# Hybrid mixer layer on one core: unstepped transposes by permuted weights, and another precedence for the decays and the first branch

## The chip, the cores and the metric

The kernel runs on one core of a Trainium2 chip. The core has a matrix engine (TensorE, "PE" in the profile, with its weight loads as "PEld"), a vector engine (VectorE, "DVE"), a scalar engine (ScalarE, "ACT"), a general engine (GpSimd, "POOL") and a queue that issues most DMAs (SyncE, "SP"). They run side by side and wait for each other through semaphores. The metric is the device time of one execution in microseconds (us); lower is better.

## The reference

One layer of a decoder on 512 tokens of 1024 channels: a gated feed-forward network (FFN), a mixer, a second FFN, a norm. All arithmetic is float32.

```python
h = x + 0.5 * swiglu(rmsnorm(h, ffn1_norm), ...)
h = h + hybrid_mixer(rmsnorm(h, mix_norm), ...)
h = h + 0.5 * swiglu(rmsnorm(h, ffn2_norm), ...)
y = rmsnorm(h, final_norm)

# hybrid_mixer
proj = u @ w_in      # hq hf hi hg | gq gk gv ga gb gz | gate_h gate_g
o_h = hgrn2_chunked(silu(hq), k_h, hi, log_f)                     # 8 heads of 128
o_h = rmsnorm(o_h, hgrn_out_norm) * silu(hg)
y_h = o_h @ w_branch_hgrn
o_g = gated_delta_chunked(q_g, k_g, cv, beta, g)                  # 16 heads of 128
o_g = rmsnorm(o_g, gdn_out_norm) * silu(gz)
y_g = o_g @ w_branch_gdn
y = sigmoid(gate_h) * y_h + sigmoid(gate_g) * y_g
return y @ w_out
```

Both branches normalise each head's 128 output channels, scale them by a gain per channel, gate them and project them back to 1024 channels. The order of the channels inside a head is free, as long as the gain, the gate and the rows of the projection use the same one.

## The kernel before

**Layout.** Activations lie with channels on the 128 partitions and tokens along the free side ("transposed"). Weights come in slabs of 128 x 512 float32; each slab is loaded into a `raw` buffer, ACT rounds it to a high part (`whi`, line 1972 in the mixer) and VectorE takes the remainder (`wlo`, line 1974). Each product is three matmuls (lines 166 to 168): high by high, high by low, low by high. A projection block of the mixer is two slabs, eight k-steps and 24 matmuls of 128 x 512.

**Stages.** The first FFN, the mixer (`mixer`), then the second FFN. In the mixer the dense work (projections of the normed input) is woven with two recurrences that run head by head:

- The first branch (HGRN2, `h_head`, eight heads i = 0 to 7): per head the gates (`h_q`, `h_f`), seven levels of products on chunks of 128 tokens (event `("S", i)` when they are done), then the chunk recurrence, squares of the output on ACT (line 1208), a scale by the norm on VectorE (line 1218, event `("o", i)`), then the output is transposed to channels on partitions and split into a high part `oh` (line 1240, ACT) and a low part (line 1243, VectorE), event `("O", i)`. For heads 4 to 7 TensorE transposes (line 1228, `pt`). For heads 0 to 3 VectorE transposes 32 x 32 blocks (`turned`, line 913), the result goes to DRAM and comes back regrouped (`regroup`, line 933). The products y0 to y7 ("branch", 8 blocks with the weights `wbh`) use all eight heads as their k-steps, in the order of the heads.
- The second branch (gated delta rule, eight pairs u = 0 to 7 of value heads): the decays of a pair (`g_e`: a broadcast DMA `gb`, eight Abs on ACT at line 1315, two Exp at line 1320), the norms of q and k (`norms`, `g_n`), the gram products (line 1385), the inverse of a triangular matrix (`g_b` on POOL, `g_inv` with matmuls at lines 1474, 1484, 1497, 1505 and copies such as line 1477 on ACT between them), the chunk recurrence (`g_rec`), then the outputs: `send` for pairs 0 to 6 (fourteen heads, VectorE transposes at line 1627, to DRAM), `keep_on` for the last pair (TensorE transposes). `operand` brings the fourteen heads back regrouped, multiplies by the gain and the gate z (line 1724) and splits. `closing` multiplies the 16 heads with `wbg`, `merged` gates and adds the two branches, and the output projection `wo` follows.

**The stepped transpose.** VectorE transposes 32 x 32 blocks. Before, the source is read with `strided`: block b takes channels b, b+4, b+8 and so on, a step of four floats. After the way through DRAM, partition 4s + b then holds channel 4s + b, the natural order.

**What sets the order of the work.** Nothing in the mixer is scheduled by the hardware's readiness: a planner (class `Desk`) runs at build time and writes the instructions of all engines in one order. Each piece of work is a generator thread with a rank; it yields the engine it needs and a cost in us (`V(n)` = 0.21 + 0.001 n for VectorE, 1.05 for a stepped transpose), a wait for events (`"on"`), a buffer (`"get"`) or a lag. At each step the planner takes, on the engine that is free first, the ready thread with the lowest rank, or with a given priority such as the trailing 1 of `yield *V(550), 1`. Each engine then executes its instructions in exactly this order, and a real delay of one instruction holds up everything behind it on that engine.

The dense blocks are taken in the order of `DENSE`; `choose` (called each time a block's first `raw` buffer is free) takes the first block whose needs are met, and z and t gates when none is. `product` then issues the blocks on TensorE in the order in which they were chosen. It has rank 9, so it fills what the heads leave; but inside a block it waits for its operands, y blocks for event `("O", k)` at step k.

Of the kernel before, what the change touches and what calls it, by code (L numbers as in the profile page):

```python
# [12 lines left out]
ALU = mybir.AluOpType  # L13
# [3 lines left out]
P = 128  # L17
T = 512
NT = T // P
D = 1024  # L20
# [6 lines left out]
VH = 16  # L27


C_F1, C_MX, C_F2, C_FN, C_HN, C_GN, C_LB, C_CV = 0, 8, 16, 24, 32, 33, 34, 50  # L30
C_N = C_CV + 32 * 4
LEVELS = (1, 2, 4, 8, 16)

DENSE = (
# [782 lines left out]
def mixer(tc, mp, e):  # L817
    nc = tc.nc
    pe, act, dve, pool, sp = nc.tensor, nc.scalar, nc.vector, nc.gpsimd, nc.sync
# [29 lines left out]
    for size, names in ((1024, "n2:2 gz:2 fs:1 ut:1"), (512, "kn:3 gm:1 qm:2 gb:2 ln:1 at:4 vb:4 t64:2 on:2"),  # L849
                        (256, "ft:1 tp:1 thg:2 x:1 we:1 s:3 w:1"), (128, "fm:1"), (64, "sm:4")):  # L850
        for it in names.split():
            n, b = it.split(":")
# [36 lines left out]
    ohd = dr.tile([HH, P, T], F32, name="ohd")  # L889
# [16 lines left out]
        return places[tag](name, shape)  # L906


    def turned(x, src, mem, then=None, *arg):


        yield "use", "DVE", 1.05
        dve.transpose(squares(x), strided(src))
        if then is not None:
            then(*arg)
        yield S
        sp.dma_start(mem, x)
        yield "lag", LAG["out"]

    def squares(x):  # L920

        return x.rearrange("p (b c s) -> p c b s", b=4, c=NT)

    def strided(x):

        x = v3(x, NT) if len(x.shape) < 3 else x
        return x.rearrange("p c (s b) -> p c b s", b=4)
# [139 lines left out]
    def h_head(i):  # L1067
# [155 lines left out]
        if i >= 4:  # L1223
            yield "get", "d", 1
            yield T_(.46)
            x = ps("pt")
            for c in range(NT):
                pe.transpose(x[:, c * P:(c + 1) * P], on[:, c], ident)
        else:
            yield "get", "ta", 1  # L1230
            x = ta("xo")
            yield from turned(x, on, ohd[i], D.put, tag_o)
            yield from regroup(x, ohd[i])
        gn = cs[:, C_HN:C_HN + 1]
        o2 = op[i]("oh", (P, 2, T), F32R)
        oh, ol = o_h[i] = o2[:, 0], o2[:, 1]
        o4 = lambda z: z.rearrange("p (c b s) -> p c b s", c=NT, b=4)
# [63 lines left out]
    def g_e(u, st):  # L1301

        yield "on", "decays", *([("at", 2 * u + 1)] if u < 2 else ["more"]), *([*R(u - 4)] if u > 3 else []), \
            *([("E", u - 1)] if u else [])
        for i in range(2):
            hd_ = 2 * u + i
            yield "get", "gb", 1
            yield S
            gb = places["gb"]("gb", (P, NT, P))
            sp.dma_start(gb, gtd[hd_:hd_ + 1].rearrange("o (c b) -> o c b", c=NT).to_broadcast([P, NT, P]))  # L1310
            yield "lag", LAG["gb"]
            a = G["at"][u % 4 * 2 + i]
            for c in range(NT):
                yield A(200)
                act.activation(a[:, c], gb[:, c], AF.Abs, bias=gam[:, c, hd_:hd_ + 1], scale=-1.0)
            D.put("gb")
        yield "use", "ACT", 3.9
        for i in range(2):
            a = G["at"][u % 4 * 2 + i]
            act.activation(a, a, AF.Exp, scale=-1.0)  # L1320
        D.fire(("E", u))
# [301 lines left out]
    def send(u, i, o):  # L1623
        yield "get", "on", 1
        x = places["on"]("on")
        yield "use", "DVE", 1.05
        dve.transpose(squares(x), strided(o))
        D.fire(("R", u, i))
        D.start((6, u), keep(od[2 * u + i], x, "on", ("od", 2 * u + i)))

# [78 lines left out]
    def operand(k, wait, get, make):  # L1709

        yield "on", *wait
        if get:
            yield "get", get, 2
        yield "on", ("od", k), *(["projected"] if k > 10 else [])
        yield "on", ("z", k)
        tag = "zo" if k > 1 else "ta"
        yield "get", tag, 1
        yield "get", "ta", 1
        og, zg = ta("og"), zos.pop(0) if k > 1 else ta("zo")
        yield S  # L1720
        sp.dma_start(zg, zd[k])
        yield from regroup(og, od[k])
        yield *V(560), 1
        dve.scalar_tensor_tensor(og, og, cs[:, C_GN:C_GN + 1], zg, op0=ALU.mult, op1=ALU.mult)
        if k > 1:
            zos.append(zg)
        D.put(tag)
        if k > 8:
            yield "on", "projected"
        yield *A(512), 1  # L1730
        a, b = so[k] = make()
        a4, b4 = (z.rearrange("p (c b s) -> p c b s", c=NT, b=4) for z in (a, b))
        act.copy(a4, squares(og))
        yield *V(512), 1
        dve.tensor_tensor(b4, squares(og), a4.bitcast(F32), op=ALU.subtract)
        D.put("ta")
        D.fire(("so", k))
# [158 lines left out]
    def choose():  # L1896
        under = sum(("f", x) in D.at and x not in D.at for x in convs)
        for x in todo:
            k, i = x
            need = {"Q": [("Q", i - 2), ("F", i - 2), *([("o", i - 4)] if i > 3 else [])] if i > 1 else [], "F": [("L", i - 4)] if i > 3 else [],  # L1900
                    "B": [("pair", i - 2)] if i > 1 else [], "D": [], "S": [],
                    "y": [("O", 5), ("o", 6), ("S", 7)], "z": ["decays"],
                    "v": ["decays"],
                    "q": [("I", i - 4)] if i > 3 else ["decays" if i < 3 else "more"],
                    "k": [("I", i - 4)] if i > 3 else ["decays" if i < 3 else "more"]}[k]
            if k == "F" and i > 5:
                need = need + [("o", i - 6)]
            if all(n in D.at for n in need) and not (k in "qkv" and under >= CONVS):
                todo.remove(x)
                return x  # L1910
        return gates.pop(0) if len(gates) > (KEEP if todo else 0) else None
# [223 lines left out]
    D.start((6, 0), second())  # L2135
    D.start((6, 0), more())
    for u in range(8):
        D.start((4, u), g_e(u, st[u]))
        D.start((4, u), g_n(u, st[u]))
        D.start((4, u, 2), g_w(u, 0, st[u]))  # L2140
        D.start((4, u, 3), g_w(u, 1, st[u]))
        D.start((3, u), g_inv(u, st[u]))
        D.start((2, u), g_rec(u, st[u]))
# [30 lines left out]
def _cols(w):  # L2174

    k, n = w.shape
    return np.ascontiguousarray(w.reshape(k // P, P, n // P, P).transpose(2, 1, 0, 3)).reshape(n // P, P, k)
# [7 lines left out]
def layout(i):  # L2185
    f = {k: np.asarray(v) for k, v in i.items()}
    x = f["x"].reshape(T, D)
    per = lambda v: v.reshape(-1, P).T
    conv = f["gdn_conv_w"][0]
    cst = np.concatenate([  # L2190
        per(f["ffn1_norm"][0]), per(f["mix_norm"][0]), per(f["ffn2_norm"][0]), per(f["final_norm"]),
        per(f["hgrn_out_norm"][0]), per(f["gdn_out_norm"][0]),
        per(f["hgrn_lb_logits"][0]), per(f["hgrn_lb_logits"][1]),
        conv.reshape(4, 32, P).transpose(2, 1, 0).reshape(P, 128)], axis=1)
    a = np.arange(P)
    sqc = np.stack([np.eye(P), a[:, None] <= a[None, :], a[None, :] < a[:, None]], 1)
    hmask = np.zeros((P, 9, 64))
    for l, hh in enumerate(LEVELS):
        g, b = np.divmod(np.arange(64), hh)
        hmask[:, l] = (a[:, None] >= 2 * hh * g) & (a[:, None] < 2 * hh * g + hh)  # L2200
    eye4 = np.eye(32).reshape(32, 8, 4).transpose(2, 0, 1)
    hmask[:, 5:] = np.tile(np.repeat(eye4, 8, axis=0), (4, 1, 1)).reshape(P, 4, 64)
    w_in = f["w_in"][0]
    off = np.cumsum([0, 1024, 1024, 1024, 1024, 1024, 1024, 2048, 16, 16, 2048, 1024, 1024])
    part = [w_in[:, off[j]:off[j + 1]] for j in range(12)]
    wt = np.concatenate([_cols(part[j]) for j in (0, 1, 4, 5, 6, 10, 11, 9)])
    vg = np.stack([_pairs(part[j]).reshape(4, P, KD, 256) for j in (2, 3)], 3)
    wn = vg.reshape(4, P, 2, 2048).transpose(0, 2, 1, 3).reshape(8, P, 2048)
    wab = np.zeros((D, 64), np.float32)
    wab[:, 0:16] = part[7]  # L2210
    wab[:, 32:48] = part[8]

    def ffn(n):
        wi, wo = f[f"ffn{n}_w_in"][0], f[f"ffn{n}_w_out"][0]
        c = _cols(wi)
        return np.stack([c[:KF], c[KF:]], 1), _cols(wo)
    w1a, w2a = ffn(1)
    w1b, w2b = ffn(2)
    out = dict(
        xT=_kpn(x.T), cst=cst, sqc=sqc, hmask=hmask,  # L2220
        dta=np.stack([f["gdn_dt_bias"][0], f["gdn_a_log"][0]], 1),
        w1o=w1a[:2].reshape(4, P, KD, P).transpose(2, 1, 0, 3).reshape(KD, P, 512),
        w1a=w1a, w2a=w2a, wm=wt[[8, 0, 9, 1]].reshape(4, P, KD, P).transpose(2, 1, 0, 3).reshape(KD, P, 512),
        wt=wt, wn=wn, wab=_kpn(wab).reshape(P, -1),
        wbh=_cols(f["w_branch_hgrn"][0]), wbg=_cols(f["w_branch_gdn"][0]), wo=_cols(f["w_out"][0]),
        w1b=w1b, w2b=w2b)
    return {k: np.ascontiguousarray(v, dtype=np.float32) for k, v in out.items()}

# [14 lines left out]
```

## Time and profile before

| what | us |
|---|---|
| median of 3 runs | 1603.14 (1601.59 to 1603.28) |
| the profiled execution, its device time | 1604.23 |
| its span, first to last instruction | 1602.4 |
| TensorE busy | 1577.6 (98%) |
| VectorE busy | 1098.7 (69%) |
| ScalarE busy | 871.8 (54%) |
| GpSimd busy | 394.0 (25%) |

All times in the text count from the first instruction of the span. "Busy" leaves out waiting and DMA-issuing instructions. Rows of groups give an instruction's line, engine, operation, the tile that it writes and those that it reads (out<-in), and its count; rows of waits name the waiting instruction, the one that released it, and total, count and longest in us. The granted clock of TensorE is 1.00 at full speed.

### The profile page before, as it was taken

What the parts mean: (1) busy time and instruction counts of PE and PEld (TensorE: products, weight loads), DVE (VectorE), ACT (ScalarE), POOL (GpSimd) and SP (SyncE); (2) the same over time, 40 slices, a digit from 0 to 9 for tenths busy, and PEclk for the clock granted to TensorE, in tenths of its full rate; (3) what the DMA queues carried; (4) which work ended last, traced back from release to release, by engine and by line L of the source; (5) the groups of instructions that cost most, each with busy time, mean ns of one, the idle gap of its engine ahead of it and who ended that gap; (6) DMA issues with size and microseconds to landing.
All of it is one profiled execution on the core that took longest, in us unless ns stands there. A gap on an engine that the chain in (4) does not pass through costs nothing.

```text
span 1602.4 us, 29214 instructions
## 1 busy us (share of the span) xinstructions
PE 1577.6 (98%) x10586; PEld 1370.3 (86%) x10586; DVE 1098.7 (69%) x1982; ACT 871.8 (54%) x1905; POOL 394.0 (25%) x736
## 2 busy tenths in 40 slices
PE   8999999999999999999999999999999999999997
PEld 7999998888878778788878888888888899999887
DVE  7877775547778768747878776556546777778243
ACT  7766664334335446447676576555325776666232
POOL 0222210100222211172541744620002322220011
PEclk9999999999999999999999999999999999999999
DMA  5988842543323225564554646746645887872343
GB/s 178 237 187 184 184 109 83 181 119 93 103 64 93 81 78 145 148 197 142 160 174 151 207 142 186 218 150 198 204 132 166 207 200 184 185 171 73 118 140 114
DMA packets 175009, 243.72 MB, mean 152 GB/s; under 512 B 40320, under 2 KB 67712, under 8 KB 174864
## 3 DMA queue, kind: packets, MB, share of 16 engines
q1 hardware_dynamic: 157296, 210.16, 42.3%
q0 software_dynamic: 17280, 31.46, 12.5%
q8 instruction: 83, 1.36, 0.3%
q14 instruction: 62, 0.51, 0.1%
q10 hardware_dynamic: 288, 0.22, 0.0%
HBM read 211.08 MB, written 30.70 MB: 151 GB/s over the span
## 4 chain that ended last, share of the span: by engine, by line
PE 60%; DVE 1%; issue 1%; DMA 1%; ACT 1%; POOL 0%; SPq 0%; POOLq 0%; DVEq 0%; ACTq 0%
PE pmm L166 13%; PE pmm L167 13%; PE pmm L168 13%; PE pfa L167 2%; PE pfa L168 2%; PE pfa L166 2%; PE pfy L168 1%; PE pfx L166 1%; PE pfy L167 1%; PE pfy L166 1%; PE pfx L167 1%; PE pfx L168 1%; PE pgq L1385 1%; PE pw L1572 1%; PE pog L1588 1%
## 5 line engine op out<-in xcount | busy, mean ns | idle before, releaser
L166 PE MATMUL pmm<-uh,whi 128*128 128x512 f32 x760 | 317.7, 418 | 5.8 <-ACT whi L709 5.7
L168 PE MATMUL pmm<-uh,wlo 128*128 128x512 f32 x760 | 298.6, 393 | 0.0
L167 PE MATMUL pmm<-ul,whi 128*128 128x512 f32 x760 | 298.5, 393 | 0.0
L1972 ACT CAST whi<-raw 128x512 fp32r<-128x512 f32 x230 | 142.6, 620 | 257.5 <-PE pmm L167 189.4
L1974 DVE TENSOR_TENSOR wlo<-raw,whi 128x512 fp32r<-128x512 f32 x230 | 162.0, 706 | 157.8 <-ACT whi L1972 151.6
L166 PEld LDWEIGHTS pmm<-uh,whi 128*128 128x128 f32 x760 | 143.9, 189 | 33.8 <-ACT whi L709 5.7
L168 PEld LDWEIGHTS pmm<-uh,wlo 128*128 128x128 f32 x760 | 143.6, 189 | 31.7
L167 PEld LDWEIGHTS pmm<-ul,whi 128*128 128x128 f32 x760 | 144.1, 190 | 25.7 <-DVE ul L193 0.2
L420 DVE TENSOR_TENSOR sig<-h,sig 128x1024 fp32r<-128x1024 f32 x80 | 97.7, 1221 | 69.9 <-ACT sig L418 69.9
L166 PE MATMUL pmm<-gh,whi 128*128 128x512 f32 (+1 forms) x374 | 140.9, 377 | 0.0
L168 PE MATMUL pmm<-gh,wlo 128*128 128x512 f32 (+1 forms) x374 | 140.9, 377 | 0.0
L167 PE MATMUL pmm<-gl,whi 128*128 128x512 f32 (+1 forms) x374 | 140.9, 377 | 0.0
L418 ACT CAST sig<-h 128x1024 fp32r<-128x1024 f32 x80 | 84.0, 1050 | 87.9 <-PE pfa L168 84.9
L204 POOL TENSOR_TENSOR acc<-acc,sqt 128x512 f32<-128x512 f32 x18 | 23.4, 1299 | 357.6 <-ACT sqt L202 357.6
L162 DVE TENSOR_TENSOR wlo<-raw,whi 128x512 fp32r<-128x512 f32 x74 | 52.9, 718 | 67.8 <-ACT whi L161 67.1
L166 PE MATMUL pfa<-th,sig 128*128 128x256 f32 x320 | 91.3, 285 | 0.4 <-ACT s L475 0.3
L168 PE MATMUL pfa<-th,sig 128*128 128x256 f32 x320 | 91.2, 285 | 0.4 <-DVE sig L420 0.4
L167 PE MATMUL pfa<-tl,sig 128*128 128x256 f32 x320 | 91.1, 285 | 0.0
L395 POOL DMA_DIRECT2D wlo<-w1b x63 | 54.5, 868 | 147.0 <-ACT s L470 102.7
L161 ACT CAST whi<-raw 128x512 fp32r<-128x512 f32 x74 | 43.9, 595 | 84.0 <-PE pmm L167 77.3
L386 ACT ACTIVATE wlo<-raw 128x512 fp32r<-128x512 f32 x120 | 75.1, 626 | 26.0 <-PE pfa L168 14.5
L395 POOL DMA_DIRECT2D wlo<-w1a x57 | 49.4, 867 | 132.7 <-ACT s L470 95.2
(502 smaller groups left out, 4247.8 us busy)
## 6 DMA issues: line engine op xcount, KB each, us to landing
raw<-wt SPq DMA_DIRECT2D x152, 256.0 KB
raw<-w1b SPq DMA_DIRECT2D x88, 256.0 KB
raw<-w1a SPq DMA_DIRECT2D x80, 256.0 KB
wlo<-w1b POOLq DMA_DIRECT2D x63, 256.0 KB, 5.4
wlo<-w1a POOLq DMA_DIRECT2D x57, 256.0 KB, 5.6
raw<-w2b SPq DMA_DIRECT2D x45, 256.0 KB
raw<-w2a SPq DMA_DIRECT2D x40, 256.0 KB
raw<-wn SPq DMA_DIRECT2D x32, 256.0 KB
```

The source lines that it names most:

```text
L161: act.copy(hi[:, :f], raw[:, :f])
L162: dve.tensor_tensor(lo[:, :f], raw[:, :f], hi[:, :f].bitcast(F32), op=ALU.subtract)
L166: pe.matmul(pt, ah, bh, start=first, stop=False, **kw)
L167: pe.matmul(pt, ah, bl, start=False, stop=False, **kw)
L168: pe.matmul(pt, al, bh, start=False, stop=last, **kw)
L204: add.tensor_tensor(acc, acc, s, op=ALU.add)
L386: act.activation(lo, raw, AF.Copy, scale=-1.0)
L395: pool.dma_start(lo, src_, accum_op=ALU.add)
L418: act.copy(hl[:, 0:2], s)
L420: dve.tensor_tensor(hl[:, 2:4], s, hl[:, 0:2].bitcast(F32), op=ALU.subtract)
L1972: act.copy(hi, raw)
L1974: dve.tensor_tensor(lo, raw, hi.bitcast(F32), op=ALU.subtract)
```

## The change

Four things:

1. The eighteen transposes (line 913 for heads 0 to 3 of the first branch, line 1627) read their source without a step, so that partition 4s + b holds channel 32b + s after the way through DRAM. To match, the rows of `wbh` for heads 0 to 3, the rows of `wbg` for heads 0 to 13, the columns of the z gates for heads 0 to 13 and two further columns of the constants `cst` (`C_HP`, `C_GP`, the two gains) are permuted by `turn`, at layout time on the host. The other transposes of line 913 (q, k and v of the delta rule) keep the step.
2. The planner's cost of these transposes falls from 1.05 to 0.72 us.
3. The blocks y0 to y7 may be chosen when head 6's levels are done (`("S", 6)`) and no longer wait for its scaled output (`("o", 6)`).
4. The threads of the decays (`g_e`) get rank 3 where they had 4.

```diff
-C_F1, C_MX, C_F2, C_FN, C_HN, C_GN, C_LB, C_CV = 0, 8, 16, 24, 32, 33, 34, 50
-C_N = C_CV + 32 * 4
+C_F1, C_MX, C_F2, C_FN, C_HN, C_GN, C_LB, C_CV, C_HP, C_GP = 0, 8, 16, 24, 32, 33, 34, 50, 178, 179
+C_N = C_CV + 32 * 4 + 2
...
-    def turned(x, src, mem, then=None, *arg):
+    def turned(x, src, mem, then=None, *arg, step=True):
...
-        yield "use", "DVE", 1.05
-        dve.transpose(squares(x), strided(src))
+        yield "use", "DVE", 1.05 if step else .72
+        dve.transpose(squares(x), strided(src) if step else src)
...
-            yield from turned(x, on, ohd[i], D.put, tag_o)
+            yield from turned(x, on, ohd[i], D.put, tag_o, step=False)
             yield from regroup(x, ohd[i])
-        gn = cs[:, C_HN:C_HN + 1]
+        gn = cs[:, C_HN:C_HN + 1] if i > 3 else cs[:, C_HP:C_HP + 1]
...
     def send(u, i, o):
-        yield "use", "DVE", 1.05
-        dve.transpose(squares(x), strided(o))
+        yield V(512)
+        dve.transpose(squares(x), o)
...
-        dve.scalar_tensor_tensor(og, og, cs[:, C_GN:C_GN + 1], zg, op0=ALU.mult, op1=ALU.mult)
+        dve.scalar_tensor_tensor(og, og, cs[:, C_GP:C_GP + 1], zg, op0=ALU.mult, op1=ALU.mult)
...
-                    "y": [("O", 5), ("o", 6), ("S", 7)], "z": ["decays"],
+                    "y": [("O", 5), ("S", 6), ("S", 7)], "z": ["decays"],
...
     for u in range(8):
-        D.start((4, u), g_e(u, st[u]))
+        D.start((3, u), g_e(u, st[u]))
...
+    turn = np.arange(P).reshape(4, 32).T.reshape(-1)
+    heads = lambda a, n: np.concatenate([a[:n * P].reshape(n, P, -1)[:, turn].reshape(n * P, -1), a[n * P:]])
...
+        per(f["hgrn_out_norm"][0])[turn], per(f["gdn_out_norm"][0])[turn]], axis=1)
...
+    part[9] = heads(part[9].T, 14).T
...
-        wbh=_cols(f["w_branch_hgrn"][0]), wbg=_cols(f["w_branch_gdn"][0]), wo=_cols(f["w_out"][0]),
+        wbh=_cols(heads(f["w_branch_hgrn"][0], 4)), wbg=_cols(heads(f["w_branch_gdn"][0], 14)), wo=_cols(f["w_out"][0]),
```

More of the change, by code (lines that the diff above doesn't have):

```diff
@@ L2193, in layout @@
         per(f["hgrn_lb_logits"][0]), per(f["hgrn_lb_logits"][1]),
[L2194 removed]
+        conv.reshape(4, 32, P).transpose(2, 1, 0).reshape(P, 128),
+        per(f["hgrn_out_norm"][0])[turn], per(f["gdn_out_norm"][0])[turn]], axis=1)
     a = np.arange(P)
```

## The prediction

> **What bounds the kernel now.** I read the page first, then the windows of the middle stage, then TensorE's waits in it.
>
> ```profile
> span 1602.4 us, 29214 instructions
> ...
> PE 1577.6 (98%) x10586; PEld 1370.3 (86%) x10586; DVE 1098.7 (69%) x1982; ACT 871.8 (54%) x1905; POOL 394.0 (25%) x736
> ```
>
> TensorE (PE) is the bound; VectorE, which the transposes run on, is at 69%. The windows below are the mixer (358 to 1240 us, the only stage whose instructions the change touches) and four stretches of 3.41 us that I need later; the columns are length, busy PE, weight loads, DVE, ACT, POOL, granted clock, DMA.
>
> ```profile
> 358.00:1240.00 882.00, 877.55 (x5860) 719.06 (x5860) 616.89 (x1322) 462.46 (x1190) 264.97 (x589) 1.00 0.49 147
> 659.27:662.68 3.41, 2.20 (x11) 1.40 (x9) 3.41 (x7) 1.29 (x2) 0.31 (x1) 1.00 0.45 107
> 662.68:666.09 3.41, 2.93 (x13) 2.47 (x14) 3.02 (x9) 1.10 (x2) 0.00 (x0) 1.00 0.38 134
> 829.93:833.34 3.41, 1.82 (x37) 1.25 (x36) 1.99 (x3) 3.16 (x11) 2.71 (x10) 1.00 0.61 211
> 833.34:836.75 3.41, 3.41 (x9) 2.62 (x8) 3.32 (x7) 2.31 (x9) 2.94 (x7) 0.50 0.27 84
> ```
>
> In 882.00 us of mixer TensorE is busy 877.55: it idles 4.45 us in all. The change adds and removes no matmul. So the mixer's time is a constant (its matmuls) plus TensorE's idle time, plus what the clock loses. The last term shows in the two lower rows: a window in which TensorE was busy only 1.82 of 3.41 us is followed by one with a granted clock of 0.50, which costs half of 3.41 = 1.7 us of matmul work. The window at 659.27, busy 2.20 of 3.41, was followed by no slow one. Between 1.21 and 1.59 us of idle time in one such window the clock falls.
>
> TensorE's waits in the mixer, the three longest (total, times, longest):
>
> ```profile
> PE pq L1484 <- ACT acc L1477: 1.6, 1, 1.6
> PE pmm L167 <- DVE oh L1243: 0.9, 1, 0.9
> PE pmm L166 <- ACT oh L1240: 0.8, 1, 0.8
> ```
>
> The first is the slow window's: 1.6 + 1.7 = 3.3 us at one place. The other two, 1.7 us together, are one place too: the first branch product waits for head 7's output. These 5.0 us are most of what any order of the mixer could give back; with all idle time gone it is 4.45 + 1.7 = 6.2 us. Nothing bounds the loss in that way: every further idle microsecond of TensorE is paid in full, since it has no slack later.
>
> **The transposes.** Four of heads 0 to 3 (xo, line 913) and fourteen of the delta outputs (line 1627, eight of them on gat) read their source with a step of four floats and will read it without a step.
>
> ```profile
> L913 DVE STREAM_TRANSPOSE xo<-hon 128x512 f32<-128x512 f32 x4 | 4.4, 1099 | 0.1
> ...
> L1457 DVE STREAM_TRANSPOSE gut<-gtp 32x256 f32<-32x256 f32 x8 | 3.5, 436 | 0.2
> ...
> L1514 DVE STREAM_TRANSPOSE gt<-gut 32x128 f32<-32x128 f32 x6 | 1.8, 303 | 0.2
> ```
>
> The two lower groups read without a step: 436 ns for 256 elements, 303 for 128, so 1.04 ns per element and 170 ns fixed, which makes 0.70 us for 512. That is 0.39 us less than 1.09, and 18 x 0.39 = 7.0 us less of VectorE. From below the saving is bounded by zero (the step might not be what costs; the unstepped rows have only 32 partitions); I take 0.39, since these are the only transposes in the trace without a step. [...] On the end it is 0 either way, since no wait in the list above ends with a transpose: TensorE's queue covers it. Without that cover it would be a gain of 0.39 us per output.
>
> The permuted weight rows, the permuted columns of the z gates and the two added columns of constants cost nothing: same number of loads, same sizes, same matmuls; the two columns ride in a load that exists.
>
> The planner is told 0.72 instead of 1.05 for these 18. Its order after the first of them (about 441 us) may shift everywhere. That is not a cost, but it redraws the small waits of the mixer.
>
> **The branch's precedence.** The first branch product y0 may be loaded when head 5's output, head 6's levels (was: head 6's finished output) and head 7's levels are planned as done. In the trace, the last step of head 7's levels (line 1150) and the last of head 6's output (line 1218) are these, with the splits (line 1974) that free a raw buffer between them:
>
> ```profile
> 620.70 0.16 DVE L1150 TENSOR_TENSOR fl<-fl 128x4 f32<-128x4 f32 x1
> 621.14 1.09 DVE L913 STREAM_TRANSPOSE xk<-h 128x512 f32<-128x512 f32 x1 [0.28 <-ACT h L1276]
> 622.16 0.65 DVE L1974 TENSOR_TENSOR wlo<-raw,whi 128x512 fp32r<-128x512 f32 x1
> 624.44 0.69 DVE L1974 TENSOR_TENSOR wlo<-raw,whi 128x512 fp32r<-128x512 f32 x1 [1.63 <-ACT whi L1972]
> ...
> 628.40 0.34 DVE L1218 SCALAR_TENSOR_TENSOR hon<-po,hrho,hg 128x128 f32<-128x128 f32 x1
> ```
>
> And the loads of weight slabs on SP's queue from 618 to 632 us (shortest, median, longest in ns; first and last start):
>
> ```profile
> L1929 SPq DMA_DIRECT2D raw<-wt x4: 328/333/346, 618.1 to 628.5; - x4
> L1929 SPq DMA_DIRECT2D raw<-wbh x1: 333/333/333, 631.1 to 631.1; - x1
> ```
>
> A block is two slabs. The four wt loads are two convolution blocks; the second of them is chosen after the split at 624.44, that is behind head 7's levels and before head 6's output. So with the new condition that choice falls on y0: **one convolution block, which stood before y0, goes behind y7**, and y0 to y7 come one block earlier. SP's queue carries the same loads in another order, and ACT and VectorE split the same number of slabs.
>
> What that does on TensorE:
>
> ```profile
> L166 PE MATMUL pmm<-oh,whi x9: 389/389/503, 655.6 to 663.7; 128*128 128x512 f32 x9
> ```
>
> ```profile
> 660.37 0.60 PE L1228 MATMUL pt<-sq,hon 128*128 128x128 f32 x4
> 661.74 0.50 PE L166 MATMUL pmm<-oh,whi 128*128 128x512 f32 x1 [0.78 <-ACT oh L1240]
> 663.16 0.50 PE L167 MATMUL pmm<-oh,whi 128*128 128x512 f32 x1 [0.92 <-DVE oh L1243]
> ```
>
> y0 begins at 655.6 and has done seven of its eight parts at 660.37: 4.77 / 7 = 0.68 us each, 5.45 a block. The eighth needs head 7's output: its transposes (pt), then oh on ACT, then its low half on VectorE, and TensorE idles 1.7 us. One block earlier, the eighth part is due at 660.37 - 5.45 = 654.92. What of head 7 can come earlier?
>
> ```profile
> 654.95 0.86 DVE L1218 SCALAR_TENSOR_TENSOR hon<-po,hrho,hg 128x128 f32<-128x128 f32 x3
> 656.23 0.69 DVE L1974 TENSOR_TENSOR wlo<-raw,whi 128x512 fp32r<-128x512 f32 x1 [0.42 <-ACT whi L1972]
> 656.84 2.31 DVE L1270 SCALAR_TENSOR_TENSOR cy<-pmm,cs,cy 128x511 f32<-128x511 f32 x3
> 659.07 0.68 DVE L1974 TENSOR_TENSOR wlo<-raw,whi 128x512 fp32r<-128x512 f32 x1
> 659.67 0.34 DVE L1218 SCALAR_TENSOR_TENSOR hon<-po,hrho,hg 128x128 f32<-128x128 f32 x1
> ```
>
> The fourth scaling stood behind the taps of exactly the block that moves away (line 1270, 2.31 us). Without them it follows the other three: 654.95 + 4 x 0.29 = 656.1, pt at about 656.3 instead of 660.37. TensorE then idles 656.3 - 654.92 = 1.4 us ahead of pt, and the 1.7 as before: 3.1 us, +1.4. Bounds: if head 7 gets no relief, 1.7 + 5.45 = 7.15, +5.45; if the plan draws head 7 ahead by the whole block, the place may cost nothing more, and 1.7 less if the wait goes. I take +1.4, nearest to the rows. 3.1 us of idle within some 4.5 us puts more than 1.59 into one window in most positions of the window, so the clock falls once: +1.7. **Sum +3.1 us.** [...]
>
> **The decays' precedence.** Thread g_e (eight Abs and two Exp per pair of heads, each with a load of function tables) goes from rank 4 to 3: ahead of the norms' squares and of the q and k convolutions' SiLU on ACT, and its gb loads ahead of the norms' on SP. What waits behind are those squares and SiLUs, and behind them the next pair's gram products. ACT is busy 462.46 of the mixer's 882.00, so that is hidden by the dense blocks that fill TensorE. What it can change is this:
>
> ```profile
> L1320 ACT ACT_TABLE_LOAD   x8: 1283/1283/1283, 571.1 to 971.5; - x8
> ```
>
> ```profile
> 828.75 1.28 ACT L1276 ACT_TABLE_LOAD   x1
> ...
> 831.15 0.34 ACT L1477 COPY acc<-pq 32x256 f32<-32x256 f32 x1
> ```
>
> The longest wait is a copy of the inverse (line 1477), late because a table load for a SiLU stood ahead of it. Eight times the Exp (line 1320) loads its table, and each time the next SiLU after it pays 1.28 us again; the plan books both with the Exp (3.9 us), not where the second happens. With Exp and SiLU in another order it falls somewhere else, and one of the eight hits TensorE now. So I let this place go: **-3.3 us**; bounds: -3.3, and 0 if another copy is hit.
>
> **Sum** for the likeliest: +3.1 - 3.3 = -0.2 us, on the profiled execution's 1604.23 us (span 1602.4 and 1.8 around it): 1604.0. The median of the runs is 1.1 below the profiled one, so 1602.9. The tail gives nothing: the merge is bound by TensorE too, and its last operands are in time:
>
> ```profile
> L166 PE MATMUL pmm<-sot,whi x4: 389/389/389, 1127.9 to 1137.0; 128*128 128x512 f32 x4
> L1652 DVE TENSOR_TENSOR ul<-zo,uh x2: 685/690/694, 1136.1 to 1138.3; 128x512 fp32r<-128x512 f32 x2
> ```
>
> The last part on sot (operand 8) begins at 1137.0. Seven parts of 0.68 us later, at 1141.8, operand 15 is due; it is ready at 1138.3 + 0.69 = 1139.0. That leaves 2.8 us, and more if y7 comes earlier; a chain that ends over 2.8 us later would be paid in full.
>
> **Rivals.** (1) *Faster: both waits shrink.* The plan brings head 7 forward or the shorter transposes let it, so that y0's wait stays under 1.2 us per window and no clock is lost, and the reload misses the inverse: between -2.6 (-3.3, and half of the 1.4) and -6.2 (no idle left): 1597 to 1600.5. For it: the longest wait hangs on an accident of order. Against it: the block ahead of y0 was cover. (2) *Slower: head 7 is not relieved.* Then y0's eighth part waits 7.15 us; two windows fall to half: +5.45 + 3.4 = +8.9 with the other wait kept, +5.6 with it gone: 1608.7 to 1612. It decides from the point at which the fourth scaling stays behind other work till 658 (+3.3 of idle time). For it: the plan gives convolutions' taps and splits precedence on VectorE; against it: the taps in its way are the moved block's. (3) *The choice does not change*, since the redrawn plan has another block's choice before head 7's levels: only small waits differ, 1600 to 1604.
>
> **How the numbers follow.** The forecast has 0.37, rival 1 0.34, rival 2 0.21, rival 3 0.08. About 0.2% (3.2 us) is what a measurement of this kernel can tell. Faster by more: rival 1 and a little of 3, 0.35. Slower by more: rival 2 and the part of the forecast in which the reload hits another copy, 0.27. Within: 0.38. The range from 1597.8 leaves out the end of rival 1, and to 1608.7 the dearer half of rival 2.
>
> **What would show it.** The 18 transposes at about 0.70 us (right) or 1.09; seven convolution blocks and not eight before the first wbh product on TensorE; its eighth part idle some 3 us, with a slow window behind it; no wait at line 1484 above 1 us. The prediction is wrong if TensorE's count of busy time in the mixer changes with the same matmuls, if head 7 is ready at y0, or if a new wait of over 2 us stands between 700 and 1140 us.

## The result, and the profile after

The changed kernel took 1597.92 us (median; 1596.1 to 1599.64), the kernel before beside it 1602.54 us (1600.46 to 1609.06). The ratio is 0.9967, with a 95% interval from 0.996 to 0.9975: a small gain, larger than the 0.2% that a measurement can tell. The forecast was 1602.9 us, no difference that a measurement can tell; the outcome is that of rival 1.

The page of the changed kernel's profile, its span and busy times:

```profile
span 1595.7 us, 29221 instructions
...
PE 1575.0 (99%) x10586; PEld 1369.9 (86%) x10586; DVE 1091.2 (68%) x1982; ACT 874.9 (55%) x1907; POOL 388.1 (24%) x736
```

VectorE has 7.5 us less (1098.7 before). TensorE has the same 10586 matmuls and is busy 99% of a shorter span. The windows of the changed kernel's mixer and of 88 us around the place where the clock fell before (columns as in the prediction):

```profile
358.00:1240.00 882.00, 881.52 (x5890) 723.80 (x5890) 614.24 (x1325) 468.16 (x1197) 261.39 (x591) 1.00 0.49 148
...
780.00:868.00 88.00, 87.83 (x564) 72.66 (x563) 71.59 (x144) 58.22 (x163) 28.44 (x79) 1.00 0.48 146
```

TensorE idles 0.48 us in 882 instead of 4.45, and the mean clock around 830 us is 1.00. The same window of the kernel before:

```profile
780.00:868.00 88.00, 86.41 (x506) 70.98 (x505) 72.83 (x146) 57.53 (x162) 43.98 (x115) 0.98 0.55 167
```

A slow window, 3.41 us at a granted clock of 0.50 (833.34 to 836.75), in 88 makes exactly this 0.98. From its first norm-sum matmul to the last matmul of `wo` the mixer took 876.68 us before and 870.63 after. In the trace 4.34 and 0.38 us of this are idle time, 1.71 and 0 are lost to the clock; what is left, the matmuls, is 870.63 and 870.26. So 5.7 of the 6.0 us are idle time and clock. The profiled spans differ by 6.7 us; the other 0.7 lie in the two FFNs, whose instructions are the same.

TensorE's waits in the changed kernel's mixer, all of them (total, times, longest):

```profile
PE pks L1559 <- DVE s L1599: 0.2, 1, 0.2
PE pmm L166 <- DVE cy L1270: 0.2, 1, 0.2
```

The inverse (line 1484), head 7's output (lines 1240, 1243) and the three smaller ones are all gone. The transposes:

```profile
L1627 DVE STREAM_TRANSPOSE on<-gat x8: 702/712/715, 789.6 to 1030.4; 128x512 f32<-128x512 f32 x8
...
L913 DVE STREAM_TRANSPOSE xo<-hon x4: 711/712/712, 442.5 to 524.8; 128x512 f32<-128x512 f32 x4
```

Before, line 913's four took 1099 ns on average (shown in the prediction), and line 1627's:

```profile
L1627 DVE STREAM_TRANSPOSE on<-gat x8: 1061/1092/1104, 793.4 to 1032.0; 128x512 f32<-128x512 f32 x8
```

0.71 us each where 1.09 to 1.10 stood: 18 x 0.39 = 7.0 us of VectorE.

**Where head 7 came from.** TensorE and VectorE of the changed kernel around y0's eighth part:

```profile
651.73 0.60 PE L1228 MATMUL pt<-sq,hon 128*128 128x128 f32 x4
...
654.92 0.39 PE L166 MATMUL pmm<-oh,whi 128*128 128x512 f32 x1
655.14 0.39 PE L167 MATMUL pmm<-oh,whi 128*128 128x512 f32 x1
```

```profile
647.69 1.12 DVE L1218 SCALAR_TENSOR_TENSOR hon<-po,hrho,hg 128x128 f32<-128x128 f32 x4
...
654.09 0.74 DVE L1243 SCALAR_TENSOR_TENSOR oh<-pt,cs,oh 128x512 fp32r<-128x512 f32 x1
```

The eighth part is due at 654.92, the very time that the prediction worked out. That is luck: another block left than the one it named. The convolution blocks up to y0 (line 1267) and the z gates (line 1683), before:

```profile
L1267 ACT ACTIVATE cy<-pmm,cs x8: 677/682/687, 609.0 to 656.1; 128x512 f32<-128x512 f32 x8
...
L1683 ACT ACTIVATE zg<-pmm x16: 577/593/602, 559.9 to 988.3; 128x512 f32<-128x512 f32 x16
```

And in the changed kernel:

```profile
L1267 ACT ACTIVATE cy<-pmm,cs x8: 671/682/687, 602.1 to 650.5; 128x512 f32<-128x512 f32 x8
...
L1683 ACT ACTIVATE zg<-pmm x16: 577/592/600, 743.3 to 985.0; 128x512 f32<-128x512 f32 x16
```

Eight convolution blocks stand ahead of y0 in both, where the forecast was seven; what is missing is the z gate at 559.9. The changed kernel's mixer also starts 1.4 us later in its trace (362.57 us, before 361.16), so counted from there the eighth part is due 1.4 us ahead of the forecast.

Head 7's transposes stand at 651.73, not at 656.3: its scaling begins at 647.69 where it began at 654.95, and its low half is ready at 654.83, 0.3 us ahead of the matmul that needs it (line 167, 655.14). The order upstream had changed. In the kernel before, the first pair's two Exp with their table load stand between head 5's scalings; ACT, then VectorE:

```profile
571.15 1.28 ACT L1320 ACT_TABLE_LOAD   x1
...
573.61 1.28 ACT L1032 ACT_TABLE_LOAD   x1
...
575.40 0.61 ACT L1972 CAST whi<-raw 128x512 fp32r<-128x512 f32 x1
```

```profile
570.59 0.86 DVE L1218 SCALAR_TENSOR_TENSOR hon<-po,hrho,hg 128x128 f32<-128x128 f32 x3
576.04 0.69 DVE L1974 TENSOR_TENSOR wlo<-raw,whi 128x512 fp32r<-128x512 f32 x1 [4.59 <-ACT whi L1972]
576.65 0.68 DVE L1974 TENSOR_TENSOR wx<-raw,wx 128x512 fp32r<-128x512 f32 x1
577.26 0.35 DVE L1218 SCALAR_TENSOR_TENSOR hon<-po,hrho,hg 128x128 f32<-128x128 f32 x1
```

Two table loads and the Exp hold ACT's rounding of a slab, VectorE idles 4.59 us behind it, and head 5's fourth scaling, queued behind that split, comes 6.7 us after the other three began. The level products of heads 6 and 7 (`pd`) begin right behind it, at 578.49. In the changed kernel the four scalings run together, and the table load of the first Exp comes 70 us later:

```profile
572.07 1.12 DVE L1218 SCALAR_TENSOR_TENSOR hon<-po,hrho,hg 128x128 f32<-128x128 f32 x4
```

```profile
L1320 ACT ACT_TABLE_LOAD  x8: 1283/1283/1283, 641.2 to 953.2; - x8
```

Counted from the mixer's start, the two groups of level products of heads 6 and 7 begin at 217.3 and 218.6 us before and at 212.3 and 214.9 in the changed kernel; head 7's scalings end at 298.8 and at 286.2. So at most 5.1 of head 7's 12.6 us are there when its levels begin. How the rest builds up on the way wasn't traced.

### The profile page after: what moved, and what is told of

It is laid out like the page before. It is cut to its first block, busy times and chain, and to the rows that moved or that the text cites. A ratio compares the mean times of both kernels' runs of the same rounds, so it can differ in the third digit from the quotient of the medians.

```text
span 1595.7 us, 29221 instructions
## 1 busy us (share of the span) xinstructions
PE 1575.0 (99%) x10586; PEld 1369.9 (86%) x10586; DVE 1091.2 (68%) x1982; ACT 874.9 (55%) x1907; POOL 388.1 (24%) x736
## 4 chain that ended last, share of the span: by engine, by line
PE 91%; DMA 3%; DVE 2%; issue 2%; ACT 1%; POOL 0%; SPq 0%; POOLq 0%; DVEq 0%; ACTq 0%
PE pmm L166 18%; PE pmm L167 17%; PE pmm L168 17%; PE pfa L166 3%; PE pfa L167 3%; PE pfa L168 3%; PE pfx L166 2%; PE pfy L168 2%; PE pfx L168 2%; PE pfx L167 2%; PE pfy L167 2%; PE pfy L166 2%; PE pnat L166 2%; PE pnat L168 2%; PE pnat L167 2%
## 5 line engine op out<-in xcount | busy, mean ns | idle before, releaser
L386 ACT ACTIVATE wlo<-raw 128x512 fp32r<-128x512 f32 x120 | 75.1, 626 | 24.8 <-PE pfa L168 12.6
```

The costliest lines, as they stand in the source:

```text
L386: act.activation(lo, raw, AF.Copy, scale=-1.0)
```

## The experiments

The theory (order): the gain is the planner's new order, whatever the transposes really take. The first rival (duration): the shorter transposes give it. The second (precedence): one of the two precedences gives it, through the wait that it was said to move. Each ratio is to the kernel before on the same chip. Idle time and clock loss are those of TensorE in the mixer in the one profiled execution, cut as above.

| run | transposes take | planner is told | branch | decays | ratio (95%) | idle, clock us |
|---|---|---|---|---|---|---|
| before | 1.09 | 1.05 | old | old | 1 | 4.3, 1.7 |
| e1_dur | 0.71 | 1.05 | old | old | 0.9996 (0.9987 to 1.0005) | 3.7, 1.7 |
| e3_y_alone | 1.09 | 1.05 | new | old | 1.0033 (1.002 to 1.0045) | 6.5, 1.7 |
| e7_both_prec | 1.09 | 1.05 | new | new | 1.0059 (1.0046 to 1.0071) | 9.3, 6.8 |
| e4_t_alone | 0.71 | 0.72 | old | old | 0.9995 (0.9986 to 1.0003) | 3.7, 0 |
| e5_no_decays | 0.71 | 0.72 | new | old | 0.9966 (0.9954 to 0.9978) | 0.0, 0 |
| e6_no_branch | 0.71 | 0.72 | old | new | 1.0034 (1.0022 to 1.0046) | 7.0, 3.4 |
| e8_after_again | 0.71 | 0.72 | new | new | 0.9971 (0.996 to 0.9981) | 0.1, 0 |
| e2_plan | 1.09 | 0.72 | new | new | 0.9972 (0.9961 to 0.9983) | 2.3, 1.7 |

### Order or duration

**e1_dur**: the data and the unstepped transposes of the changed kernel, in the order of before word for word.

```diff
-        yield "use", "DVE", 1.05 if step else .72
+        yield "use", "DVE", 1.05
...
-        yield V(512)
+        yield "use", "DVE", 1.05
         dve.transpose(squares(x), o)
```

The two precedences are put back too.

> The unstepped transposes, with the instruction order of the kernel before kept word for word (the planner is still told 1.05 us, and neither precedence is changed). Theory O (the gain is TensorE's idle time in the mixer, and that hangs on the order): the eighteen transposes take 0.71 us and not 1.09, VectorE's busy time falls by 7 us, and the time stays within 1 us of before; the waits at lines 1484, 1240 and 1243 are all still there. Theory W (the gain is VectorE's work): about -5 us, the whole gain.

1602.96 us, 0.9996. The three longest waits are those of before:

```profile
PE pq L1484 <- ACT acc L1477: 1.3, 1, 1.3
PE pmm L167 <- DVE oh L1243: 0.9, 1, 0.9
PE pmm L166 <- ACT oh L1240: 0.8, 1, 0.8
```

Seven microseconds less of VectorE are worth nothing that can be measured in the old order: the duration theory fails there.

**e2_plan**: the reverse, the order of the changed kernel with the stepped transposes and the layout of before.

```diff
-        dve.transpose(squares(x), o)
+        dve.transpose(squares(x), strided(o))
```

> The reverse: the instruction order of the kernel after word for word (the planner is told 0.72 us, both precedences changed), but the transposes keep their step and take 1.09 us. Theory O: about -5 us against before, as the kernel after; TensorE idle under 1 us in the mixer. Theory W: 0 against before. A third (the order pays only while the planner's cost is true): between, -2 to -4, with small waits behind line 1627.

1599.83 us, 0.9972: the gain, without one shorter transpose. Its only wait in the mixer:

```profile
PE pks L1559 <- DVE s L1599: 2.2, 2, 2.0
```

This wait is 0.2 us in the changed kernel; here a slow window follows it (1.7 us lost to the clock). Whether the longer transposes make it was left open by the time; e13 to e16 below take it up.

### The precedences, alone and left out

**e3_y_alone**: before, with the branch's condition alone.

```diff
-                    "y": [("O", 5), ("o", 6), ("S", 7)], "z": ["decays"],
+                    "y": [("O", 5), ("S", 6), ("S", 7)], "z": ["decays"],
```

> The kernel before with the branch's precedence alone (need of head 6's levels). In its order seven convolution blocks and not eight stand before y0. The prediction's step: TensorE idles 3.1 us at y0's eighth part instead of 1.7 (bounds 1.0 to 7.2), with the clock at half behind it: +1.4 to +3.1 at that place. Rival (head 7's chain comes forward with the order): idle 0 to 1 there, -1 to -1.7. The wait at line 1484 is redrawn in either.

1608.08 us, 1.0033: slower. Seven convolution blocks stand ahead of y0 here, as forecast, and the place that the prediction worked out can be seen in TensorE's and VectorE's timelines and in two windows:

```profile
655.35 1.10 PE L1228 MATMUL pt<-sq,hon 128*128 128x128 f32 x4 [0.27 <-DVE hon L1218]
657.23 0.49 PE L166 MATMUL pmm<-oh,whi 128*128 128x512 f32 x1 [0.78 <-ACT oh L1240]
659.20 0.50 PE L167 MATMUL pmm<-oh,whi 128*128 128x512 f32 x1 [1.48 <-DVE oh L1243]
```

```profile
654.95 1.11 DVE L1218 SCALAR_TENSOR_TENSOR hon<-po,hrho,hg 128x128 f32<-128x128 f32 x4
```

```profile
656.96:660.37 3.41, 1.67 (x6) 1.19 (x7) 3.34 (x7) 0.85 (x3) 0.00 (x0) 1.00 0.44 117
660.38:663.79 3.41, 3.41 (x10) 2.67 (x9) 2.16 (x7) 0.46 (x1) 0.00 (x0) 0.50 0.59 192
```

The fourth scaling follows the other three and ends at 656.06 (forecast 656.1); the idle time is 0.27 + 0.78 + 1.48 = 2.53 us (forecast 3.1), and one window is slow (forecast: one). Of the inverse's wait only 1.2 us is left (line 1474), with no slow window; 2.1 us at line 1586 (chunk recurrence of a pair) are new.

**e4_t_alone**: the changed kernel with both precedences as before.

```diff
-                    "y": [("O", 5), ("S", 6), ("S", 7)], "z": ["decays"],
+                    "y": [("O", 5), ("o", 6), ("S", 7)], "z": ["decays"],
...
-        D.start((3, u), g_e(u, st[u]))
+        D.start((4, u), g_e(u, st[u]))
```

> Unstepped transposes with the planner told 0.72 us, both precedences as before. In its order ten convolution blocks stand before y0 (before: eight and one z gate). If the transposes' cost in the plan alone removes the waits: -5 us. If the precedences are needed: the wait for head 7 is gone (more blocks cover it), and what is left is the draw of the inverse's copies: between -4 and 0.

1602.62 us, 0.9995. Head 7's wait and the inverse's are gone, but two others stand in their place: 2.1 us for the last operands of the merge (line 166 for line 1650) and 1.4 us at line 1385.

**e5_no_decays** and **e6_no_branch**: the changed kernel with one precedence taken back, the second or the first hunk of the diff above.

> The kernel after without the decays' precedence (rank 4 again); transposes and the branch's need as after. Up to y1 its TensorE order of dense blocks is that of the kernel after (eight convolution blocks, y0, y1). Theory O, with the wait for head 7 removed by the order up to y0: no wait at lines 1240 and 1243, mixer idle 0 to 2.5 us from the redrawn middle, -2 to -5 us against before. Rival (the decays' precedence is what clears the inverse's wait): a wait of 1 to 2 us at lines 1474 to 1505 comes back, -1 to -3.

> The kernel after without the branch's precedence; transposes and decays as after. Ten convolution blocks stand before y0 as in the run with the transposes alone, so y7 ends some 12 us later than in the kernel after, and everything that waits for the end of the branch starts later. Theory (a later branch shows as a wait for the last pair's outputs at the tail): TensorE idles 1 to 3 us at line 1650 or 1652, -1 to -3 against before. Rival (the decays' precedence makes up for it): no wait at the tail, -4 to -6.

e5: 1597.43 us, 0.9966, no wait of TensorE in the mixer at all. e6: 1608.31 us, 1.0034, with two waits:

```profile
PE pmm L166 <- ACT uh L1650: 4.1, 1, 4.1
PE pmm L166 <- ACT yh L1692: 3.0, 2, 1.5
```

So what a precedence is worth depends on what stands beside it. With the new told cost, the branch's condition gains 0.3% where the decays keep their rank (e4 0.9995, e5 0.9966) and 0.6 to 0.7% where they have the new one (e6 1.0034, e8 0.9971 and the changed kernel 0.9967); with the old cost it loses 0.33% (e3). The decays' new rank is worth nothing that can be measured beside the new condition (e5, e8) and loses 0.4% without it (e4, e6). The precedence theory in its simple form, a precedence with a worth of its own, fails.

**e7_both_prec**: before with both precedences, transposes and their cost as before.

```diff
-                    "y": [("O", 5), ("o", 6), ("S", 7)], "z": ["decays"],
+                    "y": [("O", 5), ("S", 6), ("S", 7)], "z": ["decays"],
...
-        D.start((4, u), g_e(u, st[u]))
+        D.start((3, u), g_e(u, st[u]))
```

> The kernel before with both precedences, stepped transposes and their old cost. Seven convolution blocks before y0. As with the branch's precedence alone, TensorE idles 2.5 us at y0's eighth part and the clock falls behind it; the middle is redrawn. 0 to +5 us against before. If the decays' precedence is worth something by itself it must show here: the waits at lines 1474 to 1505 and 1586 gone, and the sum at +1 or less.

1611.97 us, 1.0059. With the old cost the two precedences lose 9.2 us (1611.97 less 1602.77); the longest wait is again line 1650's, 4.4 us.

**e8_after_again**: the changed kernel once more, beside e5 to e7.

> The kernel after, beside the others on one chip: -5 us against before. Against the same order with stepped transposes (ratio 0.9972): if the order needs the short transposes, 1.5 to 3.7 us lower than that one, as its profile shows a wait of 2.0 us at line 1559 and one slow window more.

1597.71 us, 0.9971. The gain repeats.

### The named place, and other orders

**e9_exp_later**: before, where only the first pair's decays wait until head 6's output is scaled, so that their Exp cannot stand between head 5's scalings.

```diff
-            *([("E", u - 1)] if u else [])
+            *([("E", u - 1)] if u else [("o", 6)])
```

> The kernel before, with one edit: the first pair's decays wait until head 6's output is scaled, so that their Exp no longer stands on ACT between head 5's last scalings. No precedence and no transpose is changed; eight convolution blocks and one z gate stand before y0 as before. Theory H (the transposes' cost helped only by moving that Exp, which held up heads 6 and 7): heads 6 and 7 start 1 to 5 us earlier, no wait at lines 1240 and 1243 (-1.7 us), the middle redrawn: -1 to -5. Rival (heads 6 and 7 start earlier for another reason): the wait for head 7 stays at 1 us or more.

1603.26 us, 0.9988 (0.9978 to 0.9997). Head 7's wait is gone, and the inverse's as well. Head 7's scalings end 286.4 us after the mixer's start (before 298.8, changed kernel 286.2), with the eight convolution blocks and the z gate of before still ahead of y0. The edit draws other places anew too, so it isn't a clean cut, but it bears out that the Exp's place held head 7, and that the z gate did not. In exchange the merge's last operands are now late:

```profile
PE pmm L166 <- ACT uh L1650: 1.6, 2, 1.1
PE pmm L167 <- DVE ul L1652: 0.4, 2, 0.2
```

Counted from the mixer's start these operands come when they came before (line 1650 at 775.0 us, before 774.3). TensorE comes earlier, since it lost less on the way, and the 2.8 us that the prediction counted as spare are used up.

**e10_before_slack**, **e11_after_ease**, **e12_after_ease_down**: orders drawn anew by one constant of the planner that has nothing to do with the change: in before the margin `SLACK` that it keeps for TensorE, in the changed kernel the lag `EASE` behind some steps.

```diff
-SLACK = 0.8
+SLACK = 0.7
```

```diff
-EASE = 2.5
+EASE = 2.6
```

The third has 2.4 there.

> The kernel before with another constant of the planner (0.7 us instead of 0.8 as the margin of TensorE's small work); stepped transposes, old precedences. Its order has eight convolution blocks and no z gate before y0, as the kernel after has. Theory O (the gain is a matter of the order alone, and this skeleton of blocks is the good one): no wait at lines 1240 and 1243, -2 to -6 us against before. Rival (the gain needs this change): within 2 us of before.

> The kernel after with another constant of the planner (2.6 us instead of 2.5 as the lag around POOL's powers); no work is changed. Its order has a z gate and ten convolution blocks before y0, and the first Exp early as in the kernel before. If the gain is a draw of the order: it is lost in part or whole, -3 to +5 against before, with a wait of 1 to 5 us at line 1650. If it is a property of the change: -4 to -6.

> The kernel after with the same constant at 2.4 us. Its order has ten convolution blocks before y0 and no z gate, as the two runs with a late branch. Theory T (two blocks more before the branch make the last pair late): a wait of 1 to 5 us at line 1650, -2 to +5 against before. Rival (the late branch costs nothing by itself): no wait there, -4 to -6.

e10: 1597.71 us, 0.9953 (0.9941 to 0.9965), with 1.1 us idle and no slow window in the mixer: the whole gain, with none of the four edits. e11: 1617.68 us, 1.0082 (1.007 to 1.0094). e12: 1614.12 us, 1.0056 (1.0043 to 1.0069). TensorE's longest waits, in e11 and in e12:

```profile
PE pmm L166 <- ACT uh L1650: 4.4, 1, 4.4
PE pto L1643 <- ACT gqm L1620: 2.7, 1, 2.7
PE pmm L166 <- ACT yh L1692: 2.7, 1, 2.7
```

```profile
PE pmm L167 <- DVE oh L1243: 7.3, 1, 7.3
PE pks L1559 <- DVE s L1599: 2.2, 1, 2.2
```

The second has a wait of rival 2's size at rival 2's place: y0's eighth part waits 7.3 us (rival 2 had 7.15), and 5.1 us are lost to the clock (10.23 us at 0.50 from 671.08 on). But it isn't rival 2's mechanism. Head 7's scalings and its transposes are done in time (line 1228 at 665.18); its low half stands on VectorE behind a transpose that waits 5.56 us for a DMA:

```profile
674.92 1.08 DVE L913 STREAM_TRANSPOSE ggz<-h 128x512 f32<-128x512 f32 x1 [5.56 <-DMA vd<-ggz]
675.93 0.70 DVE L1243 SCALAR_TENSOR_TENSOR oh<-pt,cs,oh 128x512 fp32r<-128x512 f32 x1
```

e12 also shows that a late Exp alone doesn't bring head 7 early: there it starts 277.3 us after the mixer's start, and head 7's scalings end at 300.3.

### Are the shorter transposes worth anything in the new order?

**e13** to **e16**: four kernels with the order of the changed one, with 0, 18, 4 (first branch) and 14 (second branch) unstepped transposes; e14 is the changed kernel itself. For e15, beside the layout:

```diff
-        dve.transpose(squares(x), o)
+        dve.transpose(squares(x), strided(o))
```

and for e16:

```diff
-        dve.transpose(squares(x), strided(src) if step else src)
+        dve.transpose(squares(x), strided(src))
```

> Order of the changed kernel word for word, all eighteen transposes stepped (1.09 us), layout of before. Theory A (the order is the gain, the durations are covered): within 0.1% of the changed kernel timed beside it, and no wait over 1 us in the mixer. Theory B (the durations matter in this order): the wait at line 1559 for the second branch's chunk recurrence stands again (about 2 us) with a slow clock window, and the time is 2 to 4 us above the changed kernel's.

> The changed kernel itself, beside the others: 0.997 of the kernel before, mixer idle below 0.5 us, no wait over 0.5 us in it. Both theories expect the same; it is what the other three are compared with.

> Order of the changed kernel, only the four transposes of the first branch unstepped (0.71 us), the fourteen delta outputs stepped (1.09 us). Theory A: like the changed kernel. Theory B: the wait at line 1559 comes from the delta outputs ahead of the chunk recurrence on VectorE, so it stands here too, 2 us and a slow window: 2 to 4 us above the changed kernel.

> Order of the changed kernel, only the fourteen delta outputs unstepped (0.71 us), the four of the first branch stepped (1.09 us). Theory A: like the changed kernel. Theory B: no wait at line 1559, like the changed kernel within 1 us.

| run | unstepped | median us | ratio (95%) | mixer us | idle us |
|---|---|---|---|---|---|
| e13_order_none | 0 | 1598.2 | 0.9973 (0.9962 to 0.9984) | 871.98 | 1.58 |
| e15_order_first | 4 | 1598.42 | 0.9972 (0.9963 to 0.9982) | 871.33 | 0.77 |
| e16_order_second | 14 | 1597.19 | 0.9966 (0.9954 to 0.9978) | 870.79 | 0.71 |
| e14_order_all | 18 | 1596.04 | 0.9959 (0.9947 to 0.9972) | 869.79 | 0.05 |

The waits of e13:

```profile
PE pks L1559 <- DVE s L1599: 1.0, 2, 0.7
PE pmm L166 <- DVE cy L1270: 0.5, 1, 0.5
```

The idle time and the medians mostly fall as more transposes are short, by 1.5 and 2.2 us from end to end, but the intervals overlap. The wait at line 1559 is 1.0 us here and 2.2 in e2_plan, the same program. It isn't the fourteen alone: in e15, which has them long, it is 0.2 us. Each against the kernel before on its own chip, e2_plan and e8_after_again (0.9972 and 0.9971) show no difference. So the durations are worth between nothing and some 2 us in this order, and that stays open; the other 3 us or more (0.9973 of 1602.97 is 4.3 us for e13) are there without them.

## Why the prediction was wrong

**What bounds the kernel: right.** Constant matmuls, plus idle time, plus clock. The mixer's time less idle time and clock loss is 868.7 to 871.8 us in all traces, and every ratio goes the way of idle time and clock. Not all follow in size: e2's trace loses 2.0 us less than before and its ratio is worth 4.5; e3's loses 2.1 more and its ratio costs 5.3; e11's 20.0 and 13.2. A trace is one execution, and e2 and e13, the same program, lost 4.0 and 1.6 us in theirs. The ceiling of 6.2 us isn't contradicted: e14, with 0.05 us idle and no slow window, gained 6.9 us of the median (1602.97 less 1596.04), and its interval, 4.5 to 8.5 us, holds the ceiling.

**Transposes: right in size, and right in worth for the old order.** 0.71 us without the step (forecast 0.70), 1.09 to 1.10 with it, and worth nothing on the end in the old order (e1); in the new one between nothing and some 2 us.

**The planner's cost: the step that failed.** The prediction said that its order "may shift everywhere. That is not a cost, but it redraws the small waits of the mixer", and then worked out the branch's and the decays' places on the order of before. Its term for the branch was +3.1 us; in the changed kernel the whole wait of 1.7 us is gone and nothing is lost to the clock there. The told cost alone moves the first pair's Exp: with 1.05 (before, e1, e3, e7) it starts 211.3 us after the mixer's start, with 0.72 (the changed kernel, e2, e4, e5, e6) 279.9 or 280.0, whatever the transposes really take. The cleanest pair is e7 and e2, the same program but for the told cost: 1.0059 and 0.9972. The new place took head 5's scalings, and with them the start of heads 6 and 7, out of the Exp's way (e9 bears it out, e12 shows that it isn't all), and so the supply side of the branch's step was wrong. The told cost moved the blocks too: with it alone ten convolution blocks and no z gate stand ahead of y0 (e4), so the condition had another order to work on than the one with eight and a z gate.

**The branch's precedence: right on the order it was worked out on, wrong on the one that ran.** e3 has the place almost as forecast (2.53 us idle, one slow window). In the changed kernel the due time came out as forecast (654.92) by chance, and the wait is nought. What the prediction took for head 7's relief, the moved block's taps, is real in e3: there the scalings end 294.9 us after the mixer's start, 3.9 us earlier than before. In the changed kernel, which keeps its eight convolution blocks, they end at 286.2.

**The decays' precedence: the wait went, but not through it.** Line 1484's wait is gone in the changed kernel, in e5 without this precedence, in e9 and in e10. It hung on the order, and any redrawing lost it. Beside the new condition the edit itself is worth nothing that can be measured (e5).

**The rivals.** Rival 1 had the right outcome, 1597 to 1600.5 us, and half its mechanism: the plan brings head 7 forward, the transposes don't. Rival 2's mechanism, scalings that stay behind other work, gave no wait of that size in any run; e12's has the size from another cause. Rival 3 is out: the condition did change the choice of blocks (ten convolution blocks ahead of y0 without it in e6, eight with it).

**The signs.** Of what the prediction named as showing it, the transposes' 0.70 us and the missing wait at line 1484 came true; seven convolution blocks ahead of y0, and an idle time of some 3 us with a slow window behind it, did not, and head 7 is ready at y0.

**The tail: the 2.8 us were counted against a TensorE that still lost its 6 us.** Once it doesn't, the chain to line 1650 is late: e9 has it at its old time (775.0 us after the mixer's start) and waits for it. In e4, e6, e7 and e11, where TensorE waits for it too, the chain itself is later than before's 774.3 us (776.4, 780.9, 787.2 and 794.8). In the changed kernel that chain comes 21 us earlier (753.1 instead of 774.3), so it never shows. Which part of the new order does that wasn't traced; among the edits of this change it takes the branch's condition together with the told cost (e5: 753.3), since with either alone (e3: 765.6; e4: 776.4) it doesn't come so early; e10 has it by another constant (747.0).

What the edits of the title did: the layout made the transposes shorter, and that is at best about a third of the gain (2.2 of 6.9 us, e13 against e14); the branch's precedence belongs to the gain only beside the new told cost (e3, e4, e5), and the decays' isn't needed (e5). The gain is a better draw of the order, which another constant gives as well (e10), and which a tenth of a microsecond in yet another constant takes away, and more (e11, e12).

## What to carry to other kernels

Where a planner writes the order from told costs, a changed cost is a new order, and steps worked out on the old one hold only for an edit that leaves the old order standing: ask first what the edit redraws, and widen the range by what a neighbouring constant does (here 0.9953 to 1.0082). To know what an edit itself is worth, run it in the old order and run the new order without it; only then credit it. A spare time on the critical engine shrinks by every wait that is removed ahead of it.

## What the runs showed of the hardware

**TensorE's idle time alone did not tell after which windows the clock fell.** The prediction put the threshold between 1.21 and 1.59 us of idle time in a window of 3.41, from two windows of before. Rows of e9, then of e12, windows that lie a whole number of 3.41 us from the start of a slow stretch in the same trace, two each (the first two figures after the length are busy PE and weight loads, the sixth figure after the length is the granted clock):

```profile
1137.39:1140.80 3.41, 2.25 (x6) 1.15 (x7) 2.04 (x3) 0.69 (x2) 0.00 (x0) 1.00 0.75 262
1140.81:1144.22 3.41, 3.41 (x9) 2.64 (x8) 1.98 (x3) 0.62 (x1) 0.00 (x0) 0.50 0.29 57
```

```profile
872.47:875.88 3.41, 1.49 (x7) 1.30 (x8) 3.41 (x8) 2.26 (x12) 2.78 (x9) 1.00 0.20 75
875.88:879.29 3.41, 3.41 (x19) 2.85 (x18) 3.34 (x8) 3.24 (x6) 2.78 (x9) 1.00 0.50 126
```

In e9 the window after 1.16 us without matmuls has a clock of 0.50; in e12 the one after 1.92 us has 1.00. The busy time of the weight loads differs: 1.15 and 1.30 us. These two and six more windows of 3.41 us in the mixer, all at a clock of 1.00, by their weight loads (us):

| run | window from | busy PE | weight loads | clock in the next |
|---|---|---|---|---|
| e12 | 667.66 | 1.57 | 0.75 | 0.50 |
| e1 | 662.79 | 1.72 | 1.09 | 0.50 |
| e6 | 1138.94 | 2.19 | 1.10 | 0.50 |
| e9 | 1137.39 | 2.25 | 1.15 | 0.50 |
| e3 | 656.96 | 1.67 | 1.19 | 0.50 |
| before | 829.93 | 1.82 | 1.25 | 0.50 |
| e12 | 872.47 | 1.49 | 1.30 | 1.00 |
| before | 659.27 | 2.20 | 1.40 | 1.00 |

In these eight the clock fell after 0.75 to 1.25 us of weight loads and not after 1.30 and 1.40. That is what happened in eight windows, with the line drawn through them afterwards, and no mechanism; in the first FFN of before it doesn't hold, where the window from 0.49 us has no matmul and no weight load, and the next has a clock of 1.00. Head 7's 1.7 us of idle time lay in two windows in before, 1.21 us from 659.27 and 0.48 from 662.68, and the clock stayed at 1.00; in e1 it lay in one, 1.69 us from 662.79, and the next had 0.50, which cost 1.7 us more.

**With a source step of four floats VectorE's 32 x 32 transposes of 128 x 512 float32 took 0.39 us more than without**, 1.09 to 1.10 against 0.71 us, in the same place of the program (before and e1).
